# Token-major projections of a two-layer decoder step: the eight new tokens' block with both parts of the input in one stationary tile

## The chip, the cores and the metric

The kernel runs on one core of one Trainium2 chip. The metric is the time of one launch in device microseconds, as the median of several runs. TensorE (PE) multiplies, VectorE (DVE), ScalarE (ACT) and GpSimd (POOL) work element by element, and SyncE (SP) issues most of the loads and stores.

## What is computed

One inference step of two layers (`DEPTH = 2`) for a prompt of 1024 tokens and eight new tokens, one in each of eight sequences with 4096 tokens behind them. `D_MODEL` is 1024. Cut to what matters here, one layer is

```
h = rms_norm(x, norm_g)
(a_b, a_c, a_h, a_gate, s_q, s_k, s_v, s_gate,
 c_u, c_v, c_gate, d_q, d_k, d_v, d_gate) = jnp.split(h @ w_in, SPLIT_POINTS, axis=-1)
y_a = a_b * conv3(a_c * a_h)                      # A: gated convolution
y_b = window_attention(rope(s_q), rope(s_k), s_v) # B: 6 query heads, 2 key heads
vn  = layer_norm(c_v)                             # C: chunked spatial gating
y_c = c_u * (tril(w_spatial) @ vn + b_spatial)
y_d = dilated_attention(rope(d_q), rope(d_k), d_v)# D: three pairs of heads, dilation 1, 4, 16
proj = each y_* * silu(its gate) @ w_branch
x + sum(sigmoid(h @ w_merge) * proj) @ w_out
```

The outputs are the final hidden rows, the new convolution states, the new key and value caches and the normalised `vn` of the new tokens, all in float32. Three parts of `h @ w_in` are wanted with tokens on the partitions: `s_v` and `d_v` (128 + 384 columns, values of the attentions) and `c_v` (384 columns).

## The kernel before

Tokens are held as 1032 columns, the eight new ones first (columns 0 to 8) and the 1024 of the prompt behind. The input of a layer stands transposed in 8 k tiles of 128 x 1032. To keep float32 precision with products that round their operands, each tile is split into a high part and a low part (`hh`, `hl`, printed as `h0h`, `h0l` in layer 0 and `h1h`, `h1l` in layer 1): ACT makes the high part (L207) and DVE (L209) or, for two k tiles, POOL (L214) the low part. Weights are loaded as `wr` and split into `wh` on ACT (L154) and `wl` on POOL (L156). Each matrix product is then three products: high by high, low by high, high by low. The low by low product is left out.

Most projections are feature-major: a weight tile is stationary, and 344 columns of tokens move (L178, L181, L182), three chunks for the 1032 tokens. The token-major ones go through `tm_group` (L349): the tokens are stationary, and the weights move. A group has nine blocks, eight of 128 prompt tokens and a ninth, n = 8, of the eight new tokens. Each block takes a bank from `pacc()` and runs over 8 k tiles with three products (L367, L370, L371); a `consumer` then evicts the bank. A layer has three groups:

- `tm_v` for `s_v` and the first part of `d_v`, 256 columns; ACT scales each row by its token's 1/rms (L386) into `vn` or, for the ninth block, `vcs`;
- `c_v`, 384 columns; ACT scales (L414), DVE collects the statistics of the layer norm (L415, L416);
- `tm_v` for the rest of `d_v`, 256 columns.

Between the groups stand feature-major projections of the three query pairs of B (`qB0` ahead of the first group, `qB1` and `qB2` behind the first and the second), evicted at L281 and rotated in `rope`: DMAs swap the halves (L289), DVE multiplies by the cosines (L290), POOL by the sines (L291), DVE adds (L293; L296 and L297 where the dilated heads are reordered as well, into `dkp` and `dqp`). L552 copies the eight new tokens' columns out. Attention scores are products L519, reduced on DVE (L521) with the exponentials on ACT (L527); L501 and L506 transpose rotated keys for the cache outputs.

What sets the order: the code is written in one order, and a scheduler places each engine's instructions in its own queue at build time, so an edit of one loop can move instructions of others on every engine. Each engine works through its queue in order. Loads are tied to marks: `mark(mm)` is called on some products (in `tm_group` on the first one of blocks 0, 4 and 8, L368 and L369), and `load(dst, src, dist)` makes a load wait in the order for the mark `dist` marks back.

Of the kernel before, what the change touches and what calls it, by code (L numbers as in the profile page):

```python
# [7 lines left out]
F32 = mybir.dt.float32  # L8
F32R = mybir.dt.float32r
AF = mybir.ActivationFunctionType  # L10
ALU = mybir.AluOpType
AX = mybir.AxisListType

P = 128
DM = 1024
KT = 8
SEQ = 1024
NS = 8
T = SEQ + NS
CH = 344  # L20
NCH = 3
MIX = 384
# [10 lines left out]
def kernel(ctx: ExitStack, tc: tile.TileContext, i, o, c):  # L33
    nc = tc.nc
    pe, act, dve, pool, sp = nc.tensor, nc.scalar, nc.vector, nc.gpsimd, nc.sync
# [4 lines left out]
    tp = ctx.enter_context(tc.tile_pool(name="tp", bufs=2))  # L40
    sm = ctx.enter_context(tc.tile_pool(name="sm", bufs=1))
# [5 lines left out]
    def slot(name, dt=F32):  # L47
        return sl.tile([P, T], dt, tag="slot", name=name)
# [9 lines left out]
    def pacc():  # L58
        return psA.tile([P, 512], F32, tag="acc", name="acc")

    def pscore():
        return psS.tile([P, 512], F32, tag="sc", name="sc")

    def pmisc():
        return psM.tile([P, 512], F32, tag="ms", name="ms")

    def ctmp(name):
        return tp.tile([P, CH], F32, tag="ct", name=name, bufs=4)

    def dscr(name, shape):  # L70
        return dr.tile(shape, F32, tag=name, name=name)
# [7 lines left out]
    def mark(ins):  # L79
        marks.append(ins.ins)  # L80
        for x in [x for x in late if x[0] <= len(marks)]:
            late.remove(x)
            x[1]()
# [28 lines left out]
    def blkcols(n):  # L112
        return slice(NS + P * n, NS + P * (n + 1))
# [10 lines left out]
    for l in range(2):  # L124
# [5 lines left out]
        for b in range(NS):  # L130
# [5 lines left out]
            n = 2047 * 256 // 8  # L136
# [6 lines left out]
    def copy_piece():  # L143
        nload[0] += 1
        if pieces and nload[0] > 8:
            load(*pieces.pop(), 2)


    def split_w(shape, dmas):
        raw = wp.tile(list(shape), F32, tag="wr", name="wr", bufs=2)  # L150
        for sel, src in dmas:
            load(sel(raw), src, 4)
        hi = wp.tile(list(shape), F32R, tag="wh", name="wh", bufs=4)
        act.activation(hi, raw, AF.Copy)  # L154
        lo = wp.tile(list(shape), F32R, tag="wl", name="wl", bufs=4)
        pool.tensor_tensor(lo, raw, hi.bitcast(F32), op=ALU.subtract)  # L156
        return hi, lo
# [43 lines left out]
    def new_h(l):  # L201
        return [[slot(f"h{l}{a}_{k}", F32R) for k in range(KT)] for a in "hl"]
# [46 lines left out]
    hh, hl = new_h(0)  # L249
    xT0 = [slot(f"xT0_{k}") for k in range(KT)]  # L250
    for n0, n1 in GROUPS:
        off = NS if n0 == 0 else 0
        cs = slice(NS + n0 * P - off, NS + n1 * P)
        w = cs.stop - cs.start
        for k in range(KT):
            ks_ = slice(k * P, (k + 1) * P)
            ps = pmisc() if k % 2 else pscore()
# [12 lines left out]
    for n in range(9):  # L270
        src, M = (xin[n], P) if n < 8 else (xs, NS)
        act.activation(junk[:M, :DM], src[:M, :DM], AF.Square, accum_out=sq0[:M, n:n + 1])

    for l in range(2):
# [39 lines left out]
        else:  # L314
            pt_ = pmisc()
            for n in range(9):
                cols, M = (blkcols(n), P) if n < 8 else (slice(0, NS), NS)
# [4 lines left out]
        for n0, n1 in ((8, 9), (0, 4), (4, 8)):  # L322
            ps = pmisc()
            M = NS if n0 == 8 else P
# [5 lines left out]
            w = cs.stop - cs.start  # L330
# [17 lines left out]
        def tm_group(srcs, kk, consumer):  # L348
            N = sum(n for _, n in srcs)  # L349
            ws = []  # L350
            for k0 in range(0, KT, kk):
                dmas = []
                c0 = 0
                for col, n in srcs:
                    src = i["w_in"][l, k0 * P:(k0 + kk) * P, col:col + n].rearrange("(k p) m -> p k m", p=P)
                    dmas.append((lambda t, c0=c0, n=n: t[:, :, c0:c0 + n], src))
                    c0 += n
                ws.append(split_w([P, kk, N], dmas))
                copy_piece()
            for n in list(range(8)) + [8]:  # L360
                cols = blkcols(n) if n < 8 else slice(0, NS)
                M = P if n < 8 else NS
                ps = pacc()
                for k in range(KT):
                    hi, lo = ws[k // kk]
                    lh, ll = hh[k][:, cols], hl[k][:, cols]
                    mm = pe.matmul(ps[:M, :N], lh, hi[:, k % kk], start=(k == 0), stop=False)  # L367
                    if k == 0 and n % 4 == 0:  # L368
                        mark(mm)  # L369
                    pe.matmul(ps[:M, :N], ll, hi[:, k % kk], start=False, stop=False)  # L370
                    pe.matmul(ps[:M, :N], lh, lo[:, k % kk], start=False, stop=(k == KT - 1))  # L371
                consumer(n, M, ps[:M, :N])

        vcs = slot("vcs")
        vsam, cvs = vcs[:NS, 0:512], vcs[:NS, 512:512 + MIX]
# [37 lines left out]
        def ev_c(n, M, ps):  # L413
            act.activation(cdst(n), ps, AF.Identity, scale=rtok[:M, n:n + 1])  # L414
            dve.bn_stats(lnst[:M, n], cdst(n))  # L415
            dve.bn_aggr(lnmv[:M, n], lnst[:M, n])  # L416
        tm_group([(C_V, MIX)], 2, ev_c)
        qB.append(rope_tile(w_pair(l, S_Q, 2), "qB2"))
        tm_v([(D_V + P, 256)], 256)
# [24 lines left out]
        for n in range(9):  # L444
            M = P if n < 8 else NS
# [11 lines left out]
        for g0 in (0, 3):  # L457
            ps = pmisc()
# [6 lines left out]
        for j in range(3):  # L465
            ps = pmisc()
            pe.transpose(ps[:, :NS], cvs[:, j * P:(j + 1) * P], ident[:NS, :NS])
            dve.tensor_scalar(yC[j][:, 0:NS], ps[:, :NS], ws0[:, j:j + 1], bsps[j][:, 0:1], op0=ALU.mult, op1=ALU.add)
            for n0 in (0, 4):
                ps = pmisc()  # L470
# [43 lines left out]
        def scores(qs, ks, nk, mask, mx):  # L514

            s = tp.tile([P, 2, 256], F32, tag="s", name="s", bufs=2)
            ps = [pscore() for _ in range(2)]
            for h in range(2):
                pe.matmul(ps[h][:, :nk], qs[h], ks[h], start=True, stop=True)  # L519
            for h in range(2):  # L520
                dve.tensor_tensor_reduce(s[:, h, :nk], ps[h][:, :nk], mask, scale=0.125,  # L521
                                         scalar=-3e38, op0=ALU.add, op1=ALU.max, accum_out=mx[:, h:h + 1])
            return s
# [20 lines left out]
        def halves(t, sel):  # L544
            return [t[h * 64:(h + 1) * 64][sel] for h in range(2)]
# [13 lines left out]
        for n in range(8):  # L559
# [4 lines left out]
            for j in range(3):  # L564
                st = stB[:, n, j]
                s = scores(halves(qB[j], (slice(None), blkcols(n))), ks, nk, mask, st[:, 0:2])
# [122 lines left out]
        def ev_silu(y):  # L689

            def f(ch, cs, ps):
                g, t = ctmp("g"), ctmp("th")
                dve.tensor_tensor(g, ps, rr[:, cs], op=ALU.mult)
                act.activation(t, g, AF.Tanh, scale=0.5)
                dve.scalar_tensor_tensor(t, t, 1.0, g, op0=ALU.add, op1=ALU.mult)
                pool.tensor_tensor(y[:, cs], y[:, cs], t, op=ALU.mult)
            return f
# [121 lines left out]
        def ev_gate(sg):  # L819
            def f(ch, cs, ps):  # L820
                g, t = ctmp("g"), ctmp("th")
                dve.tensor_tensor(g, ps, rr[:, cs], op=ALU.mult)
                act.activation(t, g, AF.Tanh, scale=0.5)
                dve.scalar_tensor_tensor(sg[:, cs], t, 1.0, g, op0=ALU.add, op1=ALU.mult)
            return f
# [39 lines left out]
        ps = pmisc()  # L865
# [39 lines left out]
        for bi, n in enumerate(order):  # L905
# [9 lines left out]
            for m in range(KT):  # L915
                ms = slice(m * P, (m + 1) * P)
                if n == 1:
                    wv = i["w_branch"][l, n, :, ms].rearrange("(h j p) m -> h p j m", h=2, p=64)
                    wpj = split_w([P, 3, P], [(lambda t: t[0:64], wv[0]), (lambda t: t[64:128], wv[1])])
                else:  # L920
                    wpj = split_w([P, 3, P], [(lambda t: t,
                                               i["w_branch"][l, n, :, ms].rearrange("(j p) m -> p j m", p=P))])
                wg = w_std(i["w_merge"][l, :, n * DM + m * P:n * DM + (m + 1) * P].rearrange("(k p) m -> p k m", p=P), KT)
                if bi == 0:
                    mg[m] = slot(f"mg{m}")
                if bi == 0 and m == 0:
                    ynext = yD
                if m == 4 and bi in (1, 2):
                    ynext = load_y(order[bi + 1])
                for ch in range(NCH):  # L930
                    cs = slice(ch * CH, (ch + 1) * CH)
                    pg = pacc()
                    mm_chunk(pg, wg, KT, hh, hl, ch)
                    pp = pacc()
                    mm_chunk(pp, wpj, 3, yh, yl, ch)
                    t = ctmp("th")
                    dve.tensor_tensor(t, pg[:, :CH], rr[:, cs], op=ALU.mult)  # L937
                    act.activation(t, t, AF.Tanh, scale=0.5)  # L938
                    if bi == 0:
                        dve.scalar_tensor_tensor(mg[m][:, cs], t, 1.0, pp[:, :CH], op0=ALU.add, op1=ALU.mult)  # L940
                    else:
                        dve.scalar_tensor_tensor(t, t, 1.0, pp[:, :CH], op0=ALU.add, op1=ALU.mult)  # L942
                        pool.tensor_tensor(mg[m][:, cs], mg[m][:, cs], t, op=ALU.add)  # L943
# [37 lines left out]
        def wout(m):  # L981
            return w_std(i["w_out"][l, :, m * P:(m + 1) * P].rearrange("(k p) m -> p k m", p=P), KT)
# [20 lines left out]
        for m in range(KT - NTAIL):  # L1003
            w = wout(m)
# [16 lines left out]
        if l == 0:  # L1021
            hh, hl = nh
# [55 lines left out]
```

## Time and profile before

| | us |
|---|---|
| three runs: lowest, median, highest | 2444.09, 2444.82, 2446.32 |
| the profiled execution | 2436.83 |
| its span | 2435.1 |
| TensorE busy (products) | 2407.3 |
| DVE busy | 904.7 |
| POOL busy | 846.4 |
| ACT busy | 706.4 |

The profiled execution is 1.7 us longer than its span and 8 us shorter than the median. Layer 0 begins in the first microseconds and ends, with its output projection, around 1221 us, where the first products on `h1h` start. Its three groups lie between 48 and 162 us, those of layer 1 between 1246 and 1360. Busy time of TensorE is that of modelled, pipelined products, which overlap: the distance between the starts of two products is what one costs.

### The profile page before, as it was taken

The numbers are of one execution on the slowest core, as the hardware profiler recorded it, in microseconds if no ns is written. First come the engines' busy times: TensorE is split into PE (matmuls) and PEld (weight loads), VectorE is DVE, ScalarE is ACT, GpSimd is POOL, SyncE is SP. The second block draws the span as 40 slices with busy tenths as digits, with TensorE's granted clock in tenths as the row PEclk, the third lists the DMA queues.
The fourth block names the chain that finished last, engine by engine and source line by source line (L and its number), as shares of the span: only waits on it lengthen the run. The fifth ranks groups of instructions, "written<-read, shape, count | busy, mean of one in ns | idle before, by whom it ended". The sixth has DMA issues, their size and how long they took to land.

```text
span 2435.1 us, 38874 instructions
## 1 busy us (share of the span) xinstructions
PE 2407.3 (99%) x15896; PEld 2295.0 (94%) x15896; DVE 904.7 (37%) x1938; ACT 706.4 (29%) x1526; POOL 846.4 (35%) x556
## 2 busy tenths in 40 slices
PE   8999999999999999999999999999999999999999
PEld 7998889889999999999999988898899999999998
DVE  4456534445322122215333554443442221222153
ACT  5234532323212121214323254323222221222243
POOL 3343225342223333444433413353323234434330
PEclk9999999999999999999999999999999999999999
DMA  7242215243321222223442423352352222212232
GB/s 239 90 140 81 81 46 182 66 129 88 106 67 56 96 63 95 66 68 119 148 146 74 143 72 80 89 160 72 90 132 73 70 91 66 93 57 69 76 98 99
DMA packets 295962, 235.82 MB, mean 97 GB/s; under 512 B 52756, under 2 KB 279696, under 8 KB 293416
## 3 DMA queue, kind: packets, MB, share of 16 engines
q1 hardware_dynamic: 267952, 206.25, 28.1%
q10 hardware_dynamic: 27832, 27.10, 3.9%
q8 instruction: 125, 2.05, 0.3%
q14 instruction: 53, 0.43, 0.1%
HBM read 192.35 MB, written 76.47 MB: 110 GB/s over the span
## 4 chain that ended last, share of the span: by engine, by line
PE 96%; DVE 1%; DMA 1%; ACT 1%; POOL 0%; SPq 0%; issue 0%; ACTq 0%; POOLq 0%; DVEq 0%
PE acc L181 27%; PE acc L178 26%; PE acc L182 26%; PE acc L367 2%; PE acc L370 2%; PE acc L371 2%; PE sc L519 2%; PE ms L541 2%; PE ms L536 2%; PE ms L681 1%; DVE ml L902 0%; PE ms L474 0%; POOL qs L291 0%; DMA qs<-dk 0%; DVE dkp L297 0%; PE sc L974 0%
## 5 line engine op out<-in xcount | busy, mean ns | idle before, releaser
L156 POOL TENSOR_TENSOR wl<-wr,wh 128x384 fp32r<-128x384 f32 (+2 forms) x228 | 467.6, 2053 | 846.1 <-ACT wh L154 742.0
L181 PE MATMUL acc<-h0l,wh 128*128 128x344 f32 x1584 | 512.8, 324 | 0.0
L181 PE MATMUL acc<-h1l,wh 128*128 128x344 f32 x1584 | 512.5, 324 | 0.0
L178 PE MATMUL acc<-h0h,wh 128*128 128x344 f32 x1584 | 511.7, 323 | 0.4 <-ACT wh L154 0.3
L178 PE MATMUL acc<-h1h,wh 128*128 128x344 f32 x1584 | 511.7, 323 | 0.1
L182 PE MATMUL acc<-h0h,wl 128*128 128x344 f32 x1584 | 511.4, 323 | 0.0
L182 PE MATMUL acc<-h1h,wl 128*128 128x344 f32 x1584 | 508.7, 321 | 0.0
L154 ACT ACTIVATE wh<-wr 128x384 fp32r<-128x384 f32 (+2 forms) x228 | 205.0, 900 | 428.3 <-PE acc L181 398.2
L937 DVE TENSOR_TENSOR th<-acc,rr 128x344 f32<-128x344 f32 x192 | 99.1, 516 | 567.5 <-PE acc L182 563.9
L181 PEld LDWEIGHTS acc<-h0l,wh 128*128 128x128 f32 x1584 | 299.6, 189 | 9.8 <-issue 8.8
L181 PEld LDWEIGHTS acc<-h1l,wh 128*128 128x128 f32 x1584 | 298.8, 189 | 9.6 <-issue 8.8
L178 PEld LDWEIGHTS acc<-h0h,wh 128*128 128x128 f32 x1584 | 299.6, 189 | 4.4 <-issue 2.0
L178 PEld LDWEIGHTS acc<-h1h,wh 128*128 128x128 f32 x1584 | 298.9, 189 | 3.7 <-issue 2.0
L182 PEld LDWEIGHTS acc<-h0h,wl 128*128 128x128 f32 x1584 | 299.2, 189 | 2.3 <-issue 1.2
L182 PEld LDWEIGHTS acc<-h1h,wl 128*128 128x128 f32 x1584 | 298.7, 189 | 2.3 <-issue 1.2
L943 POOL TENSOR_TENSOR mg<-mg,th 128x344 f32<-128x344 f32 x144 | 138.1, 959 | 309.8 <-DVE th L942 309.8
L938 ACT ACTIVATE th<-th 128x344 f32<-128x344 f32 x192 | 94.3, 491 | 518.7 <-DVE th L937 518.7
L178 PE MATMUL acc<-yh,wh 128*128 128x344 f32 x576 | 184.8, 321 | 0.0
L182 PE MATMUL acc<-yh,wl 128*128 128x344 f32 x576 | 184.8, 321 | 0.0
L181 PE MATMUL acc<-yl,wh 128*128 128x344 f32 x576 | 184.8, 321 | 0.0
L181 PE MATMUL acc<-ml,wh 128*128 128x344 f32 (+3 forms) x384 | 123.1, 322 | 0.6 <-DVE ml L902 0.5
L942 DVE SCALAR_TENSOR_TENSOR th<-th,acc 128x344 f32<-128x344 f32 x144 | 73.9, 513 | 131.5 <-PE acc L182 130.8
(280 smaller groups left out, 3350.3 us busy)
## 6 DMA issues: line engine op xcount, KB each, us to landing
wr<-in_w_merge_dram SPq DMA_DIRECT2D x64, 512.0 KB
out_dram<-in_cache_dil_kv_dram SPq DMA_DIRECT2D x128, 255.9 KB
wr<-in_w_in_dram SPq DMA_DIRECT2D x60, 512.0 KB
y<-yscr SPq DMA_DIRECT2D x18, 516.0 KB
wr<-in_w_branch_dram SPq DMA_DIRECT2D x48, 192.0 KB
wr<-in_w_in_dram SPq DMA_DIRECT2D x32, 256.0 KB
wr<-in_w_out_dram SPq DMA_DIRECT2D x16, 512.0 KB
out_dram<-in_cache_dil_kv_dram SPq DMA_DIRECT2D x16, 511.0 KB
```

Of the source, the lines that this page charges most:

```text
L154: act.activation(hi, raw, AF.Copy)
L156: pool.tensor_tensor(lo, raw, hi.bitcast(F32), op=ALU.subtract)
L178: mm = pe.matmul(ps[:, :n], hi[:, k], xh[k][:, cs], start=(k == 0), stop=False)
L181: pe.matmul(ps[:, :n], hi[:, k], xl[k][:, cs], start=False, stop=False)
L182: pe.matmul(ps[:, :n], lo[:, k], xh[k][:, cs], start=False, stop=(k == kt - 1))
L367: mm = pe.matmul(ps[:M, :N], lh, hi[:, k % kk], start=(k == 0), stop=False)
L370: pe.matmul(ps[:M, :N], ll, hi[:, k % kk], start=False, stop=False)
L371: pe.matmul(ps[:M, :N], lh, lo[:, k % kk], start=False, stop=(k == KT - 1))
L937: dve.tensor_tensor(t, pg[:, :CH], rr[:, cs], op=ALU.mult)
L938: act.activation(t, t, AF.Tanh, scale=0.5)
L942: dve.scalar_tensor_tensor(t, t, 1.0, pp[:, :CH], op0=ALU.add, op1=ALU.mult)
L943: pool.tensor_tensor(mg[m][:, cs], mg[m][:, cs], t, op=ALU.add)
```

## The change

For each layer a tile `hd` of 128 x 8 x 40 is made: POOL clears it and copies, for each k tile, the eight new tokens' columns of the high part to columns 0 to 8 and those of the low part to columns 32 to 40 (16 copies of 128 x 8). In `tm_group` the ninth block has its own path. Its stationary tile is `hd[:, k]`, 40 columns, so one product with `wh` gives high by high in the bank's rows 0 to 8 and low by high in rows 32 to 40, and one with `wl` gives high by low and low by low. The 24 products of a block become 16. ACT then copies rows 32 to 40 to a temporary `sd`, DVE adds rows 0 to 8 to it, and the consumer reads `sd` in place of the bank. The ninth block carries no mark, so a group has two marks and not three. The temporaries of the tag `ct` become 384 columns wide, and the program reserves less memory for DMA descriptors, which makes room for that. From L373 on line numbers rise by 9, and from L389 on by 15.

```diff
     def ctmp(name):
-        return tp.tile([P, CH], F32, tag="ct", name=name, bufs=4)
+        return tp.tile([P, MIX], F32, tag="ct", name=name, bufs=4)[:, :CH]
...
                 M = P if n < 8 else NS
                 ps = pacc()
+                if n == 8:
+                    for k in range(KT):
+                        for a, w in enumerate(ws[k // kk]):
+                            pe.matmul(ps[:40, :N], hd[:, k], w[:, k % kk], start=(k + a == 0), stop=(k + a == KT))
+                    s = tp.tile([NS, MIX], F32, tag="ct", name="sd", bufs=4)[:, :N]
+                    act.activation(s, ps[32:32 + NS, :N], AF.Copy)
+                    dve.tensor_tensor(s, s, ps[:NS, :N], op=ALU.add)
+                    consumer(n, M, s)
+                    break
                 for k in range(KT):
...
                 consumer(n, M, ps[:M, :N])
+
+        hd = sm.tile([P, KT, 40], F32R, tag="hd", name="hd")
+        pool.memset(hd.bitcast(F32), 0.0)
+        for k in range(KT):
+            for a, h in enumerate((hh, hl)):
+                pool.tensor_copy(hd[:, k, 32 * a:32 * a + NS], h[k][:, 0:NS])
...
-    nc = bacc.Bacc("TRN2", target_bir_lowering=False, num_devices=1)
+    nc = bacc.Bacc("TRN2", target_bir_lowering=False, num_devices=1, dynamic_dma_scratch_size=1024)
```

DVE at the end of layer 0's first group, before (kB and qB_359 are the first rotations, qB_863 the next, L552 the copy of the eight new tokens):

```order
L293 TENSOR_TENSOR kB<-kB,qs 128x1032
L552 COPY qbs_1745<-kB 128x8
L293 TENSOR_TENSOR qB_359<-qB_359,qs 128x1032
L552 COPY qbs_1739<-qB_359 128x8
L290 TENSOR_TENSOR qB_863<-qB_863,cosT 128x1032
```

and after:

```order
L293 TENSOR_TENSOR kB<-kB,qs 128x1032
L567 COPY qbs_1748<-kB 128x8
L293 TENSOR_TENSOR qB_359<-qB_359,qs 128x1032
L567 COPY qbs_1742<-qB_359 128x8
L370 TENSOR_TENSOR sd<-sd,acc 8x256
L290 TENSOR_TENSOR qB_876<-qB_876,cosT 128x1032
```

The new addition, which releases the bank, stands behind both rotations.

TensorE at the end of layer 0's second group, before (L519 is the first score step):

```order
L367 MATMUL acc<-wh,h0h_135 8x384
L370 MATMUL acc<-wh,h0l_143 8x384
L371 MATMUL acc<-wl,h0h_135 8x384
L519 MATMUL sc<-kB,qB_359 128x128 x2
L178 MATMUL acc<-h0h_128,wh 128x344
L181 MATMUL acc<-h0l_136,wh 128x344
```

and after:

```order
L367 MATMUL acc<-wh,hd 40x384
L367 MATMUL acc<-wl,hd 40x384
L534 MATMUL sc<-kB,qB_359 128x128 x2
L178 MATMUL acc<-h0h_128,wh 128x344
L181 MATMUL acc<-h0l_136,wh 128x344
L178 MATMUL acc<-h0h_128,wh 128x344
L181 MATMUL acc<-h0l_136,wh 128x344
L178 MATMUL acc<-h0h_128,wh 128x344
L181 MATMUL acc<-h0l_136,wh 128x344
L534 MATMUL sc<-kB,qB_876 128x128 x2
L376 MATMUL acc<-wh,h0h_128 128x256
L379 MATMUL acc<-wh,h0l_136 128x256
```

A second score step and two products of the third group have moved up to a place six products behind the first score step.

TensorE at the transposes of the second rotated key `dkp` in layer 0, before:

```order
L182 MATMUL acc<-h0h_129,wl 128x344
L178 MATMUL acc<-h0h_130,wh 128x344
L181 MATMUL acc<-h0l_138,wh 128x344
L182 MATMUL acc<-h0h_130,wl 128x344
L501 MATMUL ms<-ident,dkp 128x128 x4
L506 MATMUL ms<-ident,dkp 8x128
```

and after:

```order
L182 MATMUL acc<-h0h_130,wl 128x344
L178 MATMUL acc<-h0h_131,wh 128x344
L181 MATMUL acc<-h0l_139,wh 128x344
L182 MATMUL acc<-h0h_131,wl 128x344
L178 MATMUL acc<-h0h_132,wh 128x344
L181 MATMUL acc<-h0l_140,wh 128x344
L182 MATMUL acc<-h0h_132,wl 128x344
L178 MATMUL acc<-h0h_133,wh 128x344
L516 MATMUL ms<-ident,dkp 128x128 x4
L521 MATMUL ms<-ident,dkp 8x128
```

The same transposes stand seven 344-column products further down (two in layer 1). The eight transposes of the third key come after as many products as before.

## Rows read from the trace of the kernel before

**Rows 1.** The page: busy time by engine, and the chain that ended last.
```profile
PE 2407.3 (99%) x15896; PEld 2295.0 (94%) x15896; DVE 904.7 (37%) x1938; ACT 706.4 (29%) x1526; POOL 846.4 (35%) x556
...
PE 96%; DVE 1%; DMA 1%; ACT 1%; POOL 0%; SPq 0%; issue 0%; ACTq 0%; POOLq 0%; DVEq 0%
```

**Rows 2.** Waits of PE: us in total, times, longest us.
```profile
PE ms L501 <- DVE dkp L297: 12.0, 4, 4.7
PE sc L259 <- DMA xs<-in_x_sample_dram: 4.4, 1, 4.4
PE ms L259 <- DVE xT L264: 2.4, 1, 2.4
```

**Rows 3.** Timeline of PE, ninth block of 256 columns: start, us, engine, line, operation.
```profile
73.05 0.28 PE L371 MATMUL acc<-wl,h0h 128*128 128x256 f32 x1
73.17 0.28 PE L367 MATMUL acc<-wh,h0h 128*8 128x256 f32 x1
...
75.81 0.28 PE L371 MATMUL acc<-wl,h0h 128*8 128x256 f32 x1
```

**Rows 4.** Timeline of PE, ninth block of 384 columns and the score step behind.
```profile
120.78 0.34 PE L367 MATMUL acc<-wh,h0h 128*8 128x384 f32 x1
...
124.77 0.33 PE L371 MATMUL acc<-wl,h0h 128*8 128x384 f32 x1
125.03 0.49 PE L519 MATMUL sc<-kB,qB 64*128 64x128 f32 x4
```

**Rows 5.** Line L367, weight loads: duration ns min/median/max, first and last start, forms.
```profile
L367 PEld LDWEIGHTS acc<-wh,h0h x216: 87/188/193, 48.0 to 161.9; 128*128 128x128 f32 x96, 128*8 128x8 f32 x12
```

**Rows 6.** Timelines of ACT, POOL, DVE and PE behind the first group.
```profile
76.82 0.45 ACT L386 ACTIVATE vcs<-acc,rtok 8x256 f32<-8x256 f32 x1
...
79.35 5.70 POOL L156 TENSOR_TENSOR wl<-wr,wh 128x768 fp32r<-128x768 f32 x2
88.26 1.85 POOL L156 TENSOR_TENSOR wl<-wr,wh 128x768 fp32r<-128x768 f32 x1 [3.21 <-ACT wh L154]
...
83.38 1.70 DVE L552 COPY qbs<-qB 128x8 f32<-128x8 f32 x1
...
87.25 0.34 PE L367 MATMUL acc<-wh,h0h 128*128 128x384 f32 x1
```

**Rows 7.** Timeline of DVE: an operation on 344 columns with a bank as input.
```profile
187.26 0.52 DVE L693 TENSOR_TENSOR g<-acc,rr 128x344 f32<-128x344 f32 x1 [0.44 <-PE acc L182]
```

**Rows 8.** Timelines of ACT, POOL and PE ahead of the third group.
```profile
131.75 1.05 ACT L154 ACTIVATE wh<-wr 128x1024 fp32r<-128x1024 f32 x1
...
132.88 5.06 POOL L156 TENSOR_TENSOR wl<-wr,wh 128x1024 fp32r<-128x1024 f32 x2 [5.09 <-ACT wh L154]
...
138.56 0.28 PE L371 MATMUL acc<-wl,h0h 128*128 128x256 f32 x1
```

**Rows 9.** Timeline of POOL: an operation of 128 x 8.
```profile
54.77 0.21 POOL L333 TENSOR_TENSOR sinT<-sinT,rr 128x8 f32<-128x8 f32 x1
```

**Rows 10.** Timelines of DVE, POOL and PE in the start.
```profile
15.06 2.30 DVE L209 SCALAR_TENSOR_TENSOR h0l<-xT,gcol,h0h 128x392 fp32r<-128x392 f32 x1 [4.04 <-ACT h0h L207]
...
18.54 0.63 DVE L209 SCALAR_TENSOR_TENSOR h0l<-xT,gcol,h0h 128x392 fp32r<-128x392 f32 x1 [0.69 <-ACT h0h L207]
...
14.60 2.35 POOL L156 TENSOR_TENSOR wl<-wr,wh 128x1024 fp32r<-128x1024 f32 x1 [1.71 <-ACT wh L154]
...
17.90 0.27 PE L259 MATMUL ms<-ident,xs 8*128 8x8 f32 x1 [2.39 <-DVE xT L264]
```

**Rows 11.** Timelines of PE and DVE at the transposes of the second rotated key.
```profile
434.20 0.32 PE L181 MATMUL acc<-h0l,wh 128*128 128x344 f32 x1
434.36 0.31 PE L182 MATMUL acc<-h0h,wl 128*128 128x344 f32 x1
436.25 0.63 PE L501 MATMUL ms<-ident,dkp 128*128 128x128 f32 x4 [1.58 <-DVE dkp L297]
...
434.14 1.97 DVE L297 TENSOR_TENSOR dkp<-dk,qs 128x1024 f32<-128x1024 f32 x1
```

## Prediction

> **What bounds the kernel now.** I read the shares of the page first, then the waits of TensorE, then single stretches of the timeline. TensorE's matmul row is busy for 2407.3 of 2435.1 us, and the chain that ended last is 96% TensorE [rows 1]. The reader should take two things from that: a product removed from TensorE's stream is worth the distance to the next product, and anything on another engine costs nothing until TensorE waits for it. TensorE's waits are few. The largest are four before L501, the transposes of a rotated key, 12.0 us in all and 4.7 at most, for the addition L297 on DVE; the next concern the input at the start [rows 2]. There is little idle time to win back, and there are few places where the other engines run close behind.
>
> **Products removed.** Each token-major group has nine blocks; the ninth, of eight tokens, has 8 k tiles with three products each. In the 256-column block the 24 products start from 73.17 to 75.81, 23 steps, so 0.115 us each [rows 3]. In the 384-column block they start from 120.78 to 124.77, 0.1735 us each [rows 4]. The change leaves 16 of 24. A 256-column block thus loses 8 x 0.115 = 0.92 us and a 384-column one 8 x 0.1735 = 1.39 us. With two of the first and one of the second in each of two layers that is 4 x 0.92 + 2 x 1.39 = **6.45 us**, all of it on the chain.
>
> This holds if a stationary tile of 40 columns is as well hidden as one of 8. The trace has no 40. Weight loads take 87 ns at 8 columns and 188 ns at 128 [rows 5], but the distance between products is 0.12 us at 128 columns (73.05 to 73.17) against 0.115 at 8 [rows 3]. The wide load is hidden behind the product before it, so 40 columns lie between 0.115 and 0.12: 0 to 16 x 0.005 = 0.08 us a block, taken as nothing, since both ends are close.
>
> A rule speaks against this. The Trainium skill ("TensorE: Matmul & The Clock Gate", section "The mechanism") says that a weight load overlaps with products in flight only where the row group differs, which it doesn't here. Its section "LDWEIGHTS" puts a load at columns / 1.2 ns: 33 ns (estimate) at 40 columns and 7 at 8. Exposed, that would take 16 x 33 - 24 x 7 = 0.36 us a block, 2.2 us in six, back from the saving. The 128-column rows, with no such gap, disagree with the rule.
>
> **The new eviction.** Before, ACT scaled the eight rows straight out of the accumulator bank (L386, 0.45 us [rows 6]). Now ACT copies rows 32 to 40 into `sd`, DVE adds the rows 0 to 8 from the bank, and ACT scales `sd`: one more ACT operation at about 0.45 us and one on DVE at most 0.52 us, as an operation on 344 columns with a bank as input takes (L693) [rows 7]. Neither engine is near full (29% and 37%) [rows 1], so the time matters only by order. ACT's scaling waits for the addition, and behind it stand a split of weights (L154) and other evictions; the bank is held until the addition ends.
>
> The first group is the place that counts. Its addition stands on DVE behind the rotation of kB and qB0, which POOL's products stretch: the last copy of these, L552, takes 1.70 us and ends at 85.08, as the two POOL weight splits end at 85.05 [rows 6]. With 0.52 us the addition ends near 85.6. The first product of the C_V group, which needs the bank, starts at 87.25 [rows 6] and comes 0.92 us earlier, at 86.3. That leaves 0.7 us: cost nothing, and every microsecond beyond is TensorE's. In the C_V group the addition stands between two short score reductions, since the second score step has been moved up there; in the third, DVE has done its long work before. Both at nothing.
>
> The moved score step puts its exponentials ahead of a weight split on ACT, which in the kernel before began at 131.75. POOL's two splits, 5.06 us together, follow from 132.88; the first of them, for k tiles 4 to 7 of the third group, is done at 132.88 + 2.53 = 135.4 and first read at 138.56, 3.1 us later [rows 8]. The split comes about 0.4 us later on ACT for the two exponentials (my estimate, from the 1.05 us that a split takes there and the shorter exponentials), and TensorE's need 1.8 us earlier: 0.92 + 1.39 saved, one score step of 0.49 [rows 4] put in. Some 0.9 us of slack is left. Bounds 0 to 1 us in each layer. For this and the similar chain in the eight tokens' attention I take **+0.3 us** in all, near nothing since each has slack by the rows; bound 4.
>
> **The new copies on POOL.** One memset and 16 copies of 128 x 8 in each layer. The nearest row is a product of 128 x 8 at 0.21 us [rows 9]: 16 x 0.21 = 3.4 us of copies a layer, with POOL at 35% [rows 1]. In layer 1 they lie among the sums of squares of the output projection, where TensorE waits for nothing, and each waits only for a tile that is made there anyway: nothing. In layer 0 they lie in the start, where TensorE does wait. There L209 on DVE takes 2.30 us from 15.06, against 0.63 at 18.54, because POOL's weight split runs from 14.60 to 16.95; TensorE's wait that ends at 17.90 follows from that [rows 10]. One or two copies right behind that split can hold DVE for 0.2 to 0.4 us more. If eight were in the way it would be 1.7 us; if none, 0. I take **+0.4 us**. The Trainium skill ("GPSIMD Engine Reference", section "Key points") says that POOL shares SBUF interfaces with VectorE where that reads two SBUF inputs. The rows agree; by that rule alone all 16 copies could hold DVE, 3.4 us, but TensorE waits for only one of those steps.
>
> **What the new order does to the waits.** Dropping the mark at n = 8 moves loads, and the scheduler refills. Before the four transposes of the second rotated key (L501) stand 7 more 344-column products in layer 0 and 2 more in layer 1 than before; the eight transposes of the third key keep their place. A product takes 0.157 us (434.20 to 434.36) [rows 11]. The 1.58 us wait before them, for L297 which ends at 436.11 [rows 11], shrinks by 7 x 0.157 = 1.1 us, and the one in layer 1, the same place, by 0.3. **-1.4 us**; bounds 0 (the rotation comes that much later too) and -3.0 (both waits gone). The 4.7 us waits stay.
>
> **The sum**, against the profiled execution's 2436.83 us: -6.45 - 1.4 + 0.4 + 0.3 = -7.15, so 2429.7. The median of the three runs is 2444.82, 8 us above the profiled one; a difference in products carries over as it is, which gives **2437.7 us**, 0.29% faster. A measurement of this kernel can tell about 0.2%, 4.9 us, from no change, so the forecast lies just outside that.
>
> **The rivals.**
> (1) The gain is paid back at the tight places: the waits before L501 don't shrink (0), the start costs 1.7, third-group splits come 1 us late in both layers (2.0). -6.45 + 3.7 = -2.75, 2442.1 us. For it: four queues are rearranged, and every slack is about 1 us. Against: the rows give a slack at each. Chance 0.25.
> (2) Slower, by one mechanism: the addition in the first group is late in both layers, because DVE's rotation runs against a further round of POOL weight splits. A round of three is 5.70 + 1.85 = 7.55 us [rows 6]; behind it the addition ends near 93.1 and TensorE, ready at 86.3, waits 6.8 us, 13.6 in two layers. -7.15 + 13.6 = +6.5, 2451.3 us. From an end at 89.9 us (3.6 a layer) the gain is gone, from 92.3 the loss passes 4.9 us. For it: DVE there already finishes with POOL. Against: the third split waits for ACT, which stands behind the addition, so it can't come first. Chance 0.13, other new waits of that size included.
> (3) The saving isn't there: if the 40-column load were exposed by half of what the rows allow, (188 - 87) / 2 = 50 ns on each of 96 products, 4.8 us go back: -2.3, 2442.5 us. Against it stands the even pace at 128 columns. Chance 0.04.
> (4) More than forecast: both short waits before L501 vanish and nothing is late: -6.45 - 3.0 = -9.5, 2435.3 us. Chance 0.10.
> The forecast has the remaining 0.48, with its own range of 2435.5 to 2440.
>
> **How the numbers follow.** Faster by over 0.2% means under 2439.9: the forecast and rival 4, 0.58. Rivals 1 and 3 make no difference that can be told, 0.29. Slower 0.13. The range runs from 2433.5, a little under rival 4, to 2448, beyond rivals 1 and 3 and halfway into rival 2, which leaves out about 0.15.
>
> **What would show it.** The ninth block should take 1.84 us at 256 columns and 2.78 at 384, at the same pace; TensorE's busy row should fall by 6 to 7 us. The wait before the four transposes should read about 0.5 and 1.2 us, the start's wait for L264, now 2.4 [rows 2], at 2.6 to 2.8. I am wrong if a new wait appears before the first product of the C_V or third group (for `sd` on DVE, or a split on ACT or POOL), or if the 40-column products step wider than 0.12 and 0.175 us.

## The result: slower by 0.85%, and the profile after

The changed kernel takes 2464.05 us, the kernel before 2444.45 us on the same chip: a ratio of 1.0085 with a 95% interval of 1.0071 to 1.0100 (the medians alone give 1.0080). I had forecast 2437.7 us, so the time went the other way by 20 us. The profiled execution has a span of 2462.5 us against 2435.1. That is 27.4 us where the medians differ by 19.6: the profile of the kernel before lies 8 us under its median, that of the changed kernel (2464.23 us) on its own.

The page of the changed kernel answers to [rows 1]; it has busy time and instructions by engine.

```profile
PE 2428.4 (99%) x15848; PEld 2309.6 (94%) x15848; DVE 924.2 (38%) x1944; ACT 707.8 (29%) x1532; POOL 865.3 (35%) x590
```

TensorE issues 48 products fewer, as it should, and is busy for 21 us more. So most of the loss isn't idle time. The waits of PE after (us in total, times, longest us) answer to [rows 2]:

```profile
PE ms L516 <- DVE dkp L297: 14.2, 3, 4.9
PE sc L259 <- DMA xs<-in_x_sample_dram: 4.7, 1, 4.7
PE ms L516 <- DVE dks L780: 4.0, 1, 4.0
PE ms L259 <- DVE xT L264: 2.4, 1, 2.4
PE acc L181 <- DVE yl L927: 1.1, 1, 1.1
```

The four waits before the transposes of the rotated keys (L501, now L516) have grown from 12.0 to 18.2 us. No wait for `sd` is in the list.

I laid the two traces side by side by counting the feature-major products (L178, L181, L182), which are the same 12,384 in both, 11,952 of them of 344 columns. The changed kernel is 2.8 us ahead at 187 us. From there to product 1601 it falls 11.5 us behind, holds that until layer 1, and loses 16 us more in the same stretch there. Summed by kind, from the start of a product to the next start without the idle time, in both layers together (the wait for the very first load is in the last line but one):

| span, us | before | after | difference |
|---|---|---|---|
| ninth blocks (144 and 96 products) | 19.7 | 13.3 | -6.4 |
| score products | 58.9 | 77.5 | +18.6 |
| idle time of TensorE | 18.5 | 24.9 | +6.4 |
| products of 344 columns | 1933.2 | 1939.1 | +5.9 |
| all else | 404.8 | 407.7 | +2.9 |
| sum | 2435.1 | 2462.5 | +27.4 |

The score products take 58.9 us in a second profile of the kernel before as well (the last run below), while its idle time and its products of 344 columns come out 3.5 us lower and 2.7 us higher. So the score row is the change's own, and the two rows under it hold a share that differs between executions. The 2.9 us of all else I haven't taken apart.

**The score products.** One group of rows by line and shape shows it: PE, 100 to 700 us, the score products of branch B with 256 keys (columns: count, busy us, mean ns, idle). The first fence is the kernel before, the second the changed one.

```profile
L519 PE MATMUL sc<-kB,qB 64*128 64x256 f32 x84 | 14.8, 428 | 0.0
```

```profile
L534 PE MATMUL sc<-kB,qB 64*128 64x256 f32 x84 | 25.1, 428 | 0.0
```

The number of products and the duration of one are the same, and yet their busy time rises by 10.3 us. Busy time counts an instant once, so fewer of them overlap. The timeline of PE at one step says why, before:

```profile
229.19 0.66 PE L536 MATMUL ms<-ident,s 128*128 128x128 f32 x4
229.78 0.70 PE L519 MATMUL sc<-kB,qB 64*128 64x256 f32 x4
230.41 0.43 PE L181 MATMUL acc<-h0l,wh 128*128 128x344 f32 x1
```

and after:

```profile
229.82 0.70 PE L534 MATMUL sc<-kB,qB 64*128 64x256 f32 x2
230.45 0.66 PE L556 MATMUL ms<-pt,v 128*64 128x128 f32 x8
231.04 0.66 PE L551 MATMUL ms<-ident,s 128*128 128x128 f32 x4
231.62 0.70 PE L534 MATMUL sc<-kB,qB 64*128 64x256 f32 x2
```

A step has the products of two heads, each contracting over 64 rows: one head's values lie on partitions 0 to 64, the other's on 64 to 128. Side by side, both heads take 0.63 us (229.78 to 230.41). In the new order the value products (L556) and the transposes (L551) of neighbouring steps stand between the heads, and each head takes 0.63 us alone. I call such a step torn. At full clock a whole step of 256 keys takes 0.633 us and a half of a torn one 0.626 everywhere in both traces, so tearing a step costs 0.62 us. In each layer five of 48 steps were torn before (two of them of 256 keys) and 20 are after (17 of 256 keys), and 15 x 0.62 = 9.3 us is what the score products gained in each layer. The Trainium skill ("TensorE: Matmul & The Clock Gate", section "The mechanism") says that products on different row groups of the array run concurrently. These rows agree where the two heads stand next to each other in the queue (0.63 us for both), and show no overlap where other products stand between (0.63 us each).

**The wait at the second rotated key.** The timelines after answer to [rows 11]:

```profile
446.41 1.09 PE L516 MATMUL ms<-ident,dkp 128*128 128x128 f32 x4 [4.93 <-DVE dkp L297]
...
442.10 2.29 DVE L296 TENSOR_TENSOR dkp<-dk,qs 128x8 f32<-128x8 f32 x1 [2.29 <-POOL qs L291]
444.31 1.96 DVE L297 TENSOR_TENSOR dkp<-dk,qs 128x1024 f32<-128x1024 f32 x1
...
438.62 3.45 POOL L291 TENSOR_TENSOR qs<-qs,sinT 128x1032 f32<-128x1032 f32 x1 [7.60 <-DMA qs<-dk]
442.03 2.33 POOL L156 TENSOR_TENSOR wl<-wr,wh 128x1024 fp32r<-128x1024 f32 x1
```

The same rows of the kernel before, where L297 follows as in [rows 11]:

```profile
434.05 0.17 DVE L296 TENSOR_TENSOR dkp<-dk,qs 128x8 f32<-128x8 f32 x1 [2.31 <-POOL qs L291]
...
434.33 4.03 POOL L156 TENSOR_TENSOR wl<-wr,wh 128x1024 fp32r<-128x1024 f32 x1 [0.31 <-ACT wh L154]
```

Before, L296 began 0.28 us ahead of POOL's next weight split and took 0.17 us; L297 began at 434.14, still ahead of the split, and the split was the one to wait (4.03 us against 2.33). After, the split starts straight behind L291, L296 stands behind it for 2.29 us, and L297 ends 2.1 us later. The split wins because the swapped halves come later: from their first DMA issue to the multiplication L290 it is 7.3 us before (423.23 to 430.50) and 9.7 after (428.93 to 438.58), so the split's other input, which was 0.31 us late before, is long ready when POOL is free. During that time the DMA engines move 290 GB/s after and 240 before (last column):

```profile
428.90:438.60 9.70, 9.70 (x63) 9.70 (x63) 0.02 (x1) 0.92 (x2) 2.12 (x1) 1.00 1.07 290
```

```profile
423.20:430.50 7.30, 7.30 (x48) 7.30 (x48) 0.00 (x0) 0.91 (x2) 2.12 (x1) 1.00 0.82 240
```

That the heavier traffic made the halves late is not shown; the last run below takes this up.

**The clock behind the wait.** Stretches of the changed kernel from 441.40 on (busy us by engine with counts, then the granted clock, DMA share, GB/s):

```profile
441.40:446.40 5.00, 0.08 (x1) 0.02 (x1) 4.30 (x3) 0.00 (x0) 3.60 (x3) 0.86 0.55 141
446.40:449.00 2.60, 2.59 (x11) 2.52 (x12) 2.60 (x2) 0.86 (x2) 2.17 (x2) 0.50 0.53 158
449.00:452.00 3.00, 3.00 (x13) 3.00 (x12) 2.91 (x4) 0.00 (x0) 0.00 (x0) 0.53 0.46 122
452.00:455.00 3.00, 3.00 (x21) 3.00 (x21) 0.62 (x2) 0.00 (x0) 0.00 (x0) 1.00 0.18 53
```

Behind the wait of 4.93 us the granted clock is 0.50, that is 1.2 GHz, and 15 products of 344 columns start 0.29 us apart and not 0.157: 2.1 us more. Before, the stretch behind the 1.58 us wait has a granted clock of 1.00.

### The profile page after: what moved, and what is told of

Its sections match the earlier page's. It is cut to its first block, busy times and chain, and to the rows that moved or that the text cites. A ratio compares the mean times of both kernels' runs of the same rounds, so it can differ in the third digit from the quotient of the medians.

```text
span 2462.5 us, 38799 instructions
## 1 busy us (share of the span) xinstructions
PE 2428.4 (99%) x15848; PEld 2309.6 (94%) x15848; DVE 924.2 (38%) x1944; ACT 707.8 (29%) x1532; POOL 865.3 (35%) x590
## 5 line engine op out<-in xcount | busy, mean ns | idle before, releaser
L156 POOL TENSOR_TENSOR wl<-wr,wh 128x384 fp32r<-128x384 f32 (+2 forms) x228 | 483.5, 2122 | 804.8 <-ACT wh L154 754.6
L178 PE MATMUL acc<-h1h,wh 128*128 128x344 f32 x1584 | 514.3, 325 | 0.1
L178 PE MATMUL acc<-h0h,wh 128*128 128x344 f32 x1584 | 513.0, 324 | 0.4 <-ACT wh L154 0.3
L181 PE MATMUL acc<-h1l,wh 128*128 128x344 f32 x1584 | 512.9, 324 | 0.0
L182 PE MATMUL acc<-h0h,wl 128*128 128x344 f32 x1584 | 512.2, 324 | 0.0
L181 PE MATMUL acc<-h0l,wh 128*128 128x344 f32 x1584 | 511.9, 323 | 0.0
L182 PE MATMUL acc<-h1h,wl 128*128 128x344 f32 x1584 | 511.1, 323 | 0.0
L178 PEld LDWEIGHTS acc<-h0h,wh 128*128 128x128 f32 x1584 | 300.0, 189 | 6.2 <-issue 4.0
L181 PEld LDWEIGHTS acc<-h0l,wh 128*128 128x128 f32 x1584 | 300.2, 190 | 5.9 <-issue 4.7
L178 PEld LDWEIGHTS acc<-h1h,wh 128*128 128x128 f32 x1584 | 300.5, 190 | 5.4 <-issue 4.0
L181 PEld LDWEIGHTS acc<-h1l,wh 128*128 128x128 f32 x1584 | 300.4, 190 | 5.5 <-issue 4.6
L182 PEld LDWEIGHTS acc<-h1h,wl 128*128 128x128 f32 x1584 | 300.3, 190 | 4.7 <-issue 3.5
L182 PEld LDWEIGHTS acc<-h0h,wl 128*128 128x128 f32 x1584 | 299.5, 189 | 4.6 <-issue 3.5
L181 PE MATMUL acc<-yl,wh 128*128 128x344 f32 x576 | 184.9, 321 | 1.1 <-DVE yl L927 1.1
L178 PE MATMUL acc<-yh,wh 128*128 128x344 f32 x576 | 184.8, 321 | 0.0
L182 PE MATMUL acc<-yh,wl 128*128 128x344 f32 x576 | 184.8, 321 | 0.0
L181 PE MATMUL acc<-ml,wh 128*128 128x344 f32 (+3 forms) x384 | 123.2, 322 | 0.5 <-DVE ml L917 0.5
```

Of the source, the lines that this page charges most:

```text
L178: mm = pe.matmul(ps[:, :n], hi[:, k], xh[k][:, cs], start=(k == 0), stop=False)
L181: pe.matmul(ps[:, :n], hi[:, k], xl[k][:, cs], start=False, stop=False)
L182: pe.matmul(ps[:, :n], lo[:, k], xh[k][:, cs], start=False, stop=(k == kt - 1))
```

## The experiments

Each count of torn steps is read from the order of that kernel. The expectations give the score products of 256 keys alone, 21.5 us a layer before and 30.8 in the changed kernel; what is measured below counts all score products, 29.4 and 38.7 us a layer.

### The mark put back

```diff
-                            pe.matmul(ps[:40, :N], hd[:, k], w[:, k % kk], start=(k + a == 0), stop=(k + a == KT))
+                            mm = pe.matmul(ps[:40, :N], hd[:, k], w[:, k % kk], start=(k + a == 0), stop=(k + a == KT))
+                            if k + a == 0:
+                                mark(mm)
```

> The changed kernel with the mark put back on the first product of the ninth block; nothing else differs in the code. In its order 84 of 96 score steps have both heads' products side by side (before 86, changed 56), and the transposes of the second key stand where they stood before (1521 and 7713 products of 344 columns ahead of them). Theory 'order' (the time went to score steps that were torn apart and to a longer wait at those transposes): 2437 to 2442 us, 3 to 7 under the kernel before; score products 21 to 23 us a layer as before (30 in the changed kernel), the wait before the transposes back to about 1.5 us. Rival 'path' (the 40-column products, the POOL copies or the addition cost the time themselves): still 2455 to 2465 us, as these are all in it.

Measured: ratio to the kernel before 1.0011 (0.9997 to 1.0024), 2445.5 us against 2441.4. The copies, the 40-column products and the addition are all in it, and the 20 us are gone, so rival "path" falls. Between the profiles of the changed kernel and this one the span shrinks by 20.5 us, 17.4 of them in the score products. The score products are back (same row as above):

```profile
L536 PE MATMUL sc<-kB,qB 64*128 64x256 f32 x84 | 15.4, 428 | 0.0
```

But 3 to 7 us of gain aren't there. The profile, with a span of 2442.0, has the 6.4 us less in the ninth blocks, and the waits at the transposes have grown as in the changed kernel:

```profile
PE ms L518 <- DVE dkp L297: 18.4, 4, 5.1
```

My expectation that they would be back at 1.5 us was a miss: the place in the order was the old one, and L296 still took 2.29 us, in both layers. The gain doesn't show in the median either; with one profile of this kernel, it is open how often its rotations come out so.

### The kernel before with the mark dropped

```diff
-                    if k == 0 and n % 4 == 0:
+                    if k == 0 and n in (0, 4):
```

> The kernel before with the mark of the ninth block dropped and the three products kept. In its order 84 of 96 score steps are side by side, and the transposes of the second key stand as far down as in the changed kernel (1528 and 7715 products). Theory 'order' in two parts: if the drop of the mark makes the longer wait there, 4 to 5 us instead of 1.5 in each layer with the half clock behind it, +6 to +11 us, 2451 to 2456, score products unchanged at 21 to 23 us a layer; if the longer wait comes with the torn steps instead, the wait shrinks as predicted and the time is 2442 to 2446.

Measured: 1.0041 (1.0027 to 1.0056), 2451.9 us. The first of the two outcomes: score products at 30.1 us a layer (22.1 for 256 keys), the waits at the second key's transposes 5.0 and 3.8 us. So the dropped mark alone costs 10 us without any of the new path. Between the profiles the span grows by 12.4 us: 5.3 in idle time, 5.9 in products of 344 columns, 3.7 of them at half clock right behind the four waits, and 1.2 in score products. It does not tear the steps (one more in each layer). Neither does the new path with the mark in place. Only both together tear 15 a layer.

### Score steps forced together, in the changed kernel and in the kernel before

```diff
+    lasttr = []
...
             for h in range(2):
-                pe.matmul(ps[h][:, :nk], qs[h], ks[h], start=True, stop=True)
+                mm = pe.matmul(ps[h][:, :nk], qs[h], ks[h], start=True, stop=True)
+                if lasttr:
+                    tc.add_manual_dep(mm.ins, lasttr[-1].name, nosync, reason="pair of heads")
...
-                    pe.transpose(ps[:, (h * kb + b) * P:(h * kb + b + 1) * P], s[:, h, b * P:(b + 1) * P], ident)
+                    tr = pe.transpose(ps[:, (h * kb + b) * P:(h * kb + b + 1) * P], s[:, h, b * P:(b + 1) * P], ident)
+            lasttr.append(tr.ins)
```

> The changed kernel with one demand more on the order: the score products of both heads of a step come behind the transposes of the step before, so all 96 steps have them side by side. The mark stays dropped. Theory 'order', with 0.42 to 0.63 us for a torn step and 40 of these in the changed kernel: 20 to 25 us under the changed kernel, 2439 to 2444 us, with score products at 19 to 20 us a layer. If only the score steps count and the wait at the second key's transposes stays, it stays above the kernel with the mark. Rival 'path': 2455 to 2465 us.

> The kernel before with the same demand as the changed kernel got: score products of both heads side by side in all 96 steps (86 in before). Theory 'order': ten torn steps at 0.42 to 0.63 us less, 4 to 6 us, 2438 to 2441 us, if the transposes of the second key (5 products further down in layer 0, 0 in layer 1) wait as long as before. Rival: a torn step costs nothing, since other products fill in: 2444.

Measured: 1.0272 (1.0255 to 1.0289) and 1.0272 (1.0256 to 1.0288), 2508 us each. Both expectations were misses by over 60 us. The demand took away the overlap of one step with the next. The longest item among the waits of PE in the first of the two:

```profile
PE ms L554 <- DVE s L595: 34.4, 16, 2.4
```

and its timeline of PE at one of them:

```profile
308.03 1.09 PE L554 MATMUL ms<-ident,s 128*128 128x128 f32 x4 [2.38 <-DVE s L595]
309.05 1.23 PE L535 MATMUL sc<-kB,qB 64*128 64x256 f32 x4
```

Sixteen waits of 2.1 to 2.4 us for the scaled exponentials of the same step come in, and the granted clock in this stretch (the third column from the end) is 0.55:

```profile
303.00:346.00 43.00, 25.80 (x135) 15.54 (x134) 16.86 (x82) 15.59 (x56) 0.00 (x0) 0.55 0.08 19
```

The score products, side by side here, take 1.23 us there and not 0.70. As a test of the torn steps the pair is inconclusive; it shows that the scheduler's order buys something for a torn step, and that the demand is no remedy.

### The waits taken out: transposes behind the first attention steps

```diff
-            cache_k(dk, f"dil_p{g}", d)
+            if g == 0:
+                cache_k(dk, "dil_p0", d)
...
                 act.activation(oview, po[:, :P], AF.Copy)
+                if g and u == 1:
+                    cache_k(dk, f"dil_p{g}", d)
```

This one move went into the kernel before, the changed kernel with the mark, and the changed kernel as it is.

> The kernel before, with one move in the code: the transposes of the second and third rotated key (L501) are written behind the first attention steps that use these keys, so in TensorE's order they stand behind 1608 and 2040 products of 344 columns and not 1521 and 1953. Theory: TensorE no longer waits there (12.0 us in the profile of before) nor runs at half clock behind these waits; some 3 to 6 us may come back as waits of the first score steps for the rotated query. 2415 to 2432 us, and a smaller spread than the kernel before. Rival: the rotation itself sets the pace, and the score steps take over the whole wait: 2438 to 2444.

> The same move on the changed kernel with the mark put back. With the waits at the transposes out of both, the difference to the run of before with late transposes is the path of the ninth block alone: theory 5 to 7 us less (48 products less are 6.45, a torn score step more in each layer gives back 1.3), so 2410 to 2427. Rival 'path': equal or slower than that run, as the copies and the addition cost what the products save.

> The same move on the changed kernel as it is, with the mark dropped and 40 torn score steps. Theory 'order': slower than the run with the mark and late transposes by the torn steps alone, 28 more by the count of halves at 0.63 us each, 17 to 19 us. Rival: what the changed kernel lost came mostly with the waits at the transposes, and the difference is under 8 us.

| transposes late, in | median, us | ratio to the kernel before | span | score products a layer | idle of TensorE |
|---|---|---|---|---|---|
| the kernel before | 2433.8 | 0.9966 (0.9954 to 0.9979) | 2431.0 | 30.7, 30.3 | 9.1 |
| the changed kernel with the mark | 2424.8 | 0.9934 (0.9918 to 0.9950) | 2423.1 | 31.2, 31.0 | 9.2 |
| the changed kernel | 2446.3 | 1.0022 (1.0009 to 1.0035) | 2449.4 | 40.2, 40.3 | 9.1 |

With idle time (without the wait for the very first load) equal in the three, the rest can be read alone. The path of the ninth block with the mark kept is worth 7.9 us between the spans and 9.0 between the medians, more than the 5 to 7 expected. Its blocks take 13.3 us in place of 19.7, and a torn step more in each layer gives 1.2 back, which makes 5.2. Another 2.5 us are products of 344 columns, of which more or fewer run at half clock: they differ by 2.7 us between the two profiles of the kernel before, too. The wider temporaries and the smaller memory for descriptors belong to this path; no run takes them apart. The torn steps cost 18.4 us in the score products, 17 to 19 expected. The medians of the two changed kernels differ by 21.5 us and the spans by 26.3, as the profile of the third kernel is the slowest of its eleven runs. Its row, where the second kernel has the 15.4 us of the run with the mark put back:

```profile
L534 PE MATMUL sc<-kB,qB 64*128 64x256 f32 x84 | 25.1, 428 | 0.0
```

The kernel before gained 7 us from late transposes (2440.7 us without them on that chip), less than expected: the range ended at 2432. TensorE's idle time falls by 9.4 us (18.5 to 9.1), since the first score steps of these keys take up 2.2 us of waits, and 8.4 us go back to score products (2.1) and to other short products (6.3, of which 3.6 are the transposes of the exponentials, L536). Products of 344 columns take only 3.1 us less (1930.2 for 1933.2). The second kernel beats both kernels of this case; it keeps the changed path, the mark and the late transposes.

### The kernel before once more

> The kernel before once more, unchanged, for a second profile. Theory 'race': in the profile shown the addition L296 on DVE began at 434.05, 0.28 us ahead of POOL's next weight split; where the swapped halves land later, the split comes first, L296 takes 2.3 us and the wait at the transposes is 3 to 5 us in place of 1.5. If the kernel before loses that race in other executions, this profile has L296 at 2.3 us in at least one of the two layers and a time above 2439; if the race is won here too, at 2436 to 2438, both L296 stand at 0.17.

Measured: 2439.4 us. L296 stands at 0.17 us at the second key in both layers, so that race was won again; the time, though, is that of the other outcome, so neither of the two that I had set out came true as a whole. At the third key it was lost once and won once (2.29 and 0.17 us; both lost in the first profile, with waits of 4.7 and 4.3 us against 4.0 and 1.7 here). The outcome changes from one execution to the next of the same kernel at that place.

The ten profiles of this case hold 40 such rotations, of the second and the third key in both layers, and they sort without exception. In 12 the multiplication L290 began 4.3 to 7.4 us behind the first issue of the swap (L289), and L296 took 0.17 us. In the 28 where it began 7.5 to 10.0 us behind, L296 took 2.3 us. The kernel before stood close to the edge, with 7.2 to 7.4 us at the second key in both of its profiles; with the mark put back it was 8.3 and 8.7 us. The traffic of the DMA engines in that time doesn't sort them: 123 to 245 GB/s in the 12, 190 to 329 in the 28. What made the halves late in the changed kernel is not shown by that rate.

## Why the prediction was wrong, step by step

**Products removed: right.** Ninth blocks after, in the timeline of PE, to be held against [rows 3] and [rows 4]:

```profile
72.84 0.28 PE L367 MATMUL acc<-wh,hd 128*40 128x256 f32 x1
72.96 0.28 PE L367 MATMUL acc<-wl,hd 128*40 128x256 f32 x1
...
74.71 0.32 PE L178 MATMUL acc<-h0h,wh 128*128 128x344 f32 x1
```

16 products in 1.87 us, 0.117 apart, where 1.84 was forecast. The six blocks save 6.4 us for 6.45. A load of 40 columns takes 114 ns and is hidden, and rival 3 is out. The rule of the Trainium skill that I set against it ("TensorE: Matmul & The Clock Gate", section "The mechanism", loads overlap only where row groups differ) doesn't hold here, taken alone. I had left out that the same section also lets a load be pulled ahead into a background weight buffer; the hidden loads fit that, and no run here shows the buffer itself.

**The new eviction: right.** In the first group the addition runs as predicted behind both rotations, and the first product that needs its bank doesn't wait:

```profile
83.69 0.40 DVE L370 TENSOR_TENSOR sd<-sd,acc 8x256 f32<-8x256 f32 x1
...
86.09 0.34 PE L376 MATMUL acc<-wh,h0h 128*128 128x384 f32 x1
```

It ends at 84.1, 1.5 us earlier than I had put it, with 2.0 us of slack. Rival 2, the slower one, was about this place and isn't what made the kernel slower. The longest wait of TensorE's products for this addition in any run is 0.8 us, in the changed kernel with late transposes.

**The copies on POOL: nothing, for the 0.4 us taken.** A copy takes 0.19 us. L209 takes 2.30 us as in [rows 10] and TensorE's wait there is 2.39 us in both. The weight splits ahead of the third group cost no wait either.

**What the new order does to the waits: this step failed, twice.** First, I asked of the moved instructions where they stand and what they wait for, and not which products stand next to each other. The sum prices the products that are removed and the waits, and takes every product that stays at its old cost, in the rivals too: the moved score step counts only for its exponentials and its 0.49 us. The order shows a score step as one row of two products where it is whole and as two rows where it is torn, and the excerpts above show whole ones only; the 0.63 us was in the trace of before too, where five steps a layer are torn. That is the missing term of +18.6 us, and it is why TensorE's busy row rose by 21.1 us where a fall of 6 to 7 was forecast. None of the signs that I had named for being wrong appeared: no new wait before the second or third group, and steps of 0.117 and 0.175 us. Second, the waits grew where the sum has them shrink: from 12.0 to 18.2 us at the transposes of the rotated keys. I let the wait before the second key's transposes shrink by the products inserted (-1.4 us, bounds 0 and -3.0), as if the rotation's end were fixed. Counted from the last eviction of the key (422.76 before, 428.46 after) the rotation ended 4.5 us later, since the swapped halves came 2.4 us later and the race that this lost took 2.1, and the half clock came on top; the bounds had no plus side. The margin to see was 0.28 us between L296 and POOL's split. The waits of 4.7 us that I said would stay are 4.9 and 4.3 after.

**The sum's base.** I took the 8 us between the profiled execution and the median as a shift that carries over. The waits at the transposes differ between executions of one kernel (12.0 and 8.8 us in the two profiles of the kernel before), so a base that holds them needn't carry over to a change that moves them. The kernel with the mark has the predicted saving, and its median is no better than that of the kernel before: all four of its waits at the transposes are long in its profile, and those of the kernel before were short at the second key in both of its profiles. The saving came to light only where these waits were out.

**What stays open.** Why the scheduler tears the steps only when the shorter block and the dropped mark come together; the runs show that, and not the rule inside it. Why the swapped halves come later in the changed orders, with the mark dropped or kept. Also why products of 344 columns start 0.29 us apart for some microseconds in stretches without waits, at places that differ between runs.

## What to carry to other kernels

Where two half-height products run side by side, a change of order can double them without a single wait: compare the busy time of each group of equal count, and look for neighbours that were pulled apart. Here a saving of 6.4 us in products was smaller than the 18.6 us that the order cost, so keep the things that steer the order (here a mark) when the work that carried them changes, and take waits out on their own so that the saving can be seen.

## What the hardware showed that I hadn't expected

- The products of two heads, 64 rows each and 256 columns in float32, take 0.63 us together when adjacent and 0.63 us each when other products stand between them.
- Between DVE and POOL, in these rows, the one that started first held the other: where L296 began 0.28 us ahead of POOL's split it took 0.17 us and not 2.29, and the split, behind L297, took 4.03 us and not 2.33.
- A wait of 4.93 us was followed by 5.4 us at a granted clock of about 0.5 (446.4 to 451.8); one of 1.58 us by none.
